# Attention: the probabilities are divided by their sums inside the transpose, as a float32 product with a diagonal matrix

## The chip, the cores and the metric

The kernel runs on one core of a Trainium2 chip. A core has TensorE (PE; its weight loads are listed apart as PEld), VectorE (DVE), ScalarE (ACT), GpSimd (POOL) and SyncE (SP), each with an instruction queue of its own that runs in order, and 16 DMA engines. Two memories matter here: SBUF, and PSUM, into which PE writes. The metric is the time of one execution in device microseconds; the time before is the median of three runs. The profile is one execution, recorded by the hardware profiler.

## The reference, cut to what matters

A trunk of two layers over two request groups, a prompt of 1024 tokens and a sample of 512, with 1024 features: a Fourier mixer and a SwiGLU channel mixer, then grouped-query attention (8 query heads, 2 key heads, 128 features a head) and a second SwiGLU. The change is in the attention, where each row of probabilities is divided by its sum:

```python
def block(qi):
    sc = jnp.einsum('bqkgd,bskd->bkgqs', qi, k).astype(jnp.float32) * scale
    p = jax.nn.softmax(sc, axis=-1).astype(v.dtype)
    return jnp.einsum('bkgqs,bskd->bqkgd', p, v)
```

All is float32, as input and as output.

## The kernel before

The 1536 tokens are three blocks of 512 columns: block 0 is the sample, blocks 1 and 2 are the prompt. Most products are made from operands split into a high and a low part of a reduced format (float32r), in three matmuls (`mm3`, lines 247 to 249: high by high, high by low, low by high). `split` makes the two parts: ACT casts the high part (line 240), and DVE, or POOL where it is told so, subtracts it (line 241). Weights come by SP's DMA queue into `raw` and are split by ACT (line 278) and POOL (line 279).

A few products are left in plain float32: a filler loop of 36 products at the start (line 262), sums over partitions with a column of ones (lines 299 and 1021, four products a time), and `in_rows`, which spreads a column over rows by a product of ones with four diagonal tiles (ACT makes the diagonal from `ident` in line 307, PE multiplies in line 308). Transposes go through PE with `ident` as the moving operand (lines 1003 and 1088).

Two programs are woven together by estimated costs (`weave`): the main one is the channel mixer (`ffn`), whose matmuls are the bulk of the work; the other is attention with its projections. `attend((0,))` runs for the sample and `attend((1, 2))` for the prompt. What the code writes in this woven order is then put into each engine's queue by the framework's scheduler, which may move instructions past each other.

Inside `attend`, for each of 8 heads and each block of 128 query rows (4 blocks a head for the sample, 8 for the prompt, 96 in all):

- `scores` multiplies queries and keys into a PSUM tile `a` (one `mm3` for each 512 keys; one buffer of two banks), takes the row maximum (DVE, line 1070), scales it (DVE, line 1071), makes the exponentials `p` with their row sums (ACT, line 1074), inverts the sums (DVE, line 1075) and multiplies `p` by the inverse in place (ACT, line 1076). `p` has two buffers.
- `turned`, one block later, transposes `p` in pieces of 128x128, four to a PSUM bank `c` (PE, line 1088), and splits the result into `pt` (ACT line 240, DVE line 241). A block has one such group of four for the sample and two for the prompt: 32 x 1 + 64 x 2 = 160 groups, 640 transposes.
- `values`, after every second block, multiplies `pt` with the values (matmuls of 256 columns), copies the result to a tile `t` from the four rotating buffers `tX` (ACT, line 1099) and sends it out by SP's queue (line 1100).

In the profile's names, `g`, `c` and `a` are PSUM banks, `h` and `mid` the mixer's operands, `acc` its accumulators, `col` small columns, and `t` rotating tiles.

Of the kernel before, what the change touches and what calls it, by code (L numbers as in the profile page):

```python
# [13 lines left out]
AF = mybir.ActivationFunctionType  # L14
ALU = mybir.AluOpType
AX = mybir.AxisListType

P = 128
# [106 lines left out]
def trunk_kernel(ctx: ExitStack, tc: tile.TileContext, t: dict):  # L125
    nc = tc.nc
    act, dve, pool, pe, sp = nc.scalar, nc.vector, nc.gpsimd, nc.tensor, nc.sync
# [34 lines left out]
    def tl(name, shape, dt, tag, pool_=None):  # L162
        pool_ = pool_ or pools["sbX" if tag[-1] in "XB" else "sbF"]
        return pool_.tile([P, *shape], dt, tag=tag, name=nm(name), bufs=BUFS[tag])
# [11 lines left out]
    def w_tile(*shape):  # L176
        return tl("w", shape, F32R, "w" + cur[0])
# [4 lines left out]
    def raw_tile(*shape):  # L182
        return tl("raw", shape, F32, "raw" + cur[0])

    def tmp(n=TB, dt=F32):
        return tl("t", [n], dt, "t" + cur[0])

    def bank():
        return tl("c", [TB], F32, "c" + cur[0], pools["ps" + cur[0]])

    def bank2():
        return tl("a", [2, TB], F32, "gX", pools["psX"])
# [14 lines left out]
    def acc_tile(name, shape, dt):  # L207
        return tl(name, shape, dt, "acc", accp)

    def col(n):  # L210
        return cols.tile([P, n], F32, tag=f"col{n}{cur[0]}", name=nm("col"))


    ident = cp.tile([P, P], F32, name="ident")
# [21 lines left out]
    def split(hi, lo, src, gain=None, eng=None):  # L236

        eng = eng or dve
        if gain is None:
            act.copy(hi, src)  # L240
            eng.tensor_tensor(lo, src, hi.bitcast(F32), op=ALU.subtract)  # L241
        else:
            act.activation(hi, src, AF.Copy, scale=gain)
            eng.scalar_tensor_tensor(lo, src, gain, hi.bitcast(F32), op0=ALU.mult, op1=ALU.subtract)

    def mm3(out, lh, ll, rh, rl, first, last):
        pe.matmul(out, lh, rh, start=first, stop=False)  # L247
        pe.matmul(out, lh, rl, start=False, stop=False)  # L248
        pe.matmul(out, ll, rh, start=False, stop=last)  # L249
# [787 lines left out]
    def attend(blocks):  # L1037
        nb = len(blocks)
        T = nb * TB
        nk = T // P  # L1040
        for g in range(NKV):
            kt, vt = w_tile(2, T), w_tile(2, nk, HD)
            kr = raw_tile(T)
            for n, b in enumerate(blocks):
                sp.dma_start(kr[:, n * TB : (n + 1) * TB], dqk[b][NH + g][:, :])
            split(kt[:, 0], kt[:, 1], kr, eng=pool)
            yield 1.0
            vr = raw_tile(nk, HD)
            for n, b in enumerate(blocks):
                sp.dma_start(vr[:, n * 4 : n * 4 + 4], dv[b][g][:, :, :])  # L1050
            split(vt[:, 0], vt[:, 1], vr, eng=pool)
            yield 1.0
            for h in range(g * GROUP, (g + 1) * GROUP):
                qr = raw_tile(T)
                for n, b in enumerate(blocks):
                    sp.dma_start(qr[:, n * TB : (n + 1) * TB], dqk[b][h][:, :])
                qt = w_tile(2, T)
                split(qt[:, 0], qt[:, 1], qr, eng=pool)
                pts = {}

                def scores(qc):
                    qs = slice(qc * P, (qc + 1) * P)
                    sc = bank2()
                    for kb in range(nb):
                        ks = slice(kb * TB, (kb + 1) * TB)
                        mm3(sc[:, kb], qt[:, 0, qs], qt[:, 1, qs], kt[:, 0, ks], kt[:, 1, ks], True, True)
                    s_in = sc[:, 0:nb].rearrange("p b n -> p (b n)")
                    gq = 4 * blocks[0] + qc
                    st = col(3)
                    dve.tensor_reduce(st[:, 0:1], s_in, op=ALU.max, axis=AX.X)  # L1070
                    dve.tensor_tensor(st[:, 1:2], st[:, 0:1], nrqc[:, gq, h : h + 1], op=ALU.mult)  # L1071
                    sm = col(2)
                    p = tl("p", [T], F32, "pX", ap)
                    act.activation(p, s_in, AF.Exp, bias=st[:, 1:2], scale=rqc[:, gq, h : h + 1], accum_out=sm[:, 0:1])
                    dve.reciprocal(sm[:, 1:2], sm[:, 0:1])
                    act.activation(p, p, AF.Copy, scale=sm[:, 1:2])
                    return p

                def turned(qc, p):
                    if qc % 2 == 0:  # L1080
                        pts[qc // 2] = [acc_tile("pt", [2, 4, 256], F32R) for _ in range(nk // 4)]
                    pt = pts[qc // 2]
                    qo = slice((qc % 2) * P, (qc % 2) * P + P)
                    for kq in range(nk // 4):
                        tr = bank()
                        for i in range(4):
                            kc = kq * 4 + i
                            pe.transpose(tr[:, i * P : (i + 1) * P], p[:, kc * P : (kc + 1) * P], ident)  # L1088
                        trv = tr.rearrange("p (i n) -> p i n", i=4)
                        split(pt[kq][:, 0, :, qo], pt[kq][:, 1, :, qo], trv)  # L1090

                def values(u):
                    pt = pts.pop(u)
                    po = bank()
                    for kc in range(nk):
                        mm3(po[:, 0:256], vt[:, 0, kc], vt[:, 1, kc], pt[kc // 4][:, 0, kc % 4], pt[kc // 4][:, 1, kc % 4], kc == 0, kc == nk - 1)
                    n, c0 = divmod(u * 256, TB)
                    o = tmp(256)
                    act.copy(o, po[:, 0:256])
                    sp.dma_start(dot[blocks[n]][:, h, c0 : c0 + 256], o)  # L1100

                last = None
                for qc in range(nk + 1):
                    p = scores(qc) if qc < nk else None
                    yield 0.7 * nb
                    if qc:
                        turned(qc - 1, last)
                        yield 0.8 * nb
                        if qc % 2 == 0:
                            values(qc // 2 - 1)  # L1110
                            yield 0.8 * nb
                    last = p
# [28 lines left out]
    turned = []  # L1141
# [89 lines left out]
    def aux_1():  # L1231
        yield from qkv(0, kept[0])
        yield from attend((0,))
        yield from prepare(2, 0)
# [6 lines left out]
    def aux_3():  # L1241
        yield from paced(qkv(2, kept[2]), 0.4)
        yield from paced(attend((1, 2)), 0.65)
        for b in (1, 2):
            yield from paced(out_projection(b), 0.5)
        close_pool("ap")
        close_pool("sbX")
        tp = open_pool("mT")
        for name in ("B11", "B21", "T2", "T1", "B22"):
            ops[name] = tl(name, [2, 4, TB], F32R, "mT", tp)  # L1250
        yield from moving((1, 2), g_ffn[1], ops)
        close_pool("psX")
        last["pair"] = ffn_pair(1, (1, 2), ops, t["y"])
        cur[0] = "F"
        v = next(last["pair"])
        cur[0] = "X"
        yield v

    last = {}
# [100 lines left out]
```

## Time and profile before

| what | before |
|---|---|
| median of 3 runs (lowest to highest) | 3047.74 us (3045.54 to 3047.97) |
| profiled execution, its own time | 3047.57 us |
| its span, first to last instruction | 3045.8 us |
| mean granted clock of PE | 0.995 |
| line 1074, exponentials, 128x1024 x64 and 128x512 x32 | 77.5 and 24.9 us of ACT |
| line 1075, reciprocals, x96 | 15.2 us of DVE |
| line 240, casts of `pt`, x160 | 88.6 us of ACT |
| line 241, subtractions for `pt`, x160 | 106.9 us of DVE |

The profile's page gives, for each engine, the busy time and its share of the span. The chain of work that ended last follows the last instruction back, step by step, to what released it; its shares say which engine set the end. A row of the table of groups has line, engine, operation, names (out<-in), shapes and count, then busy time, mean duration of one in ns, and the engine's idle time just before these instructions with what ended it. A row of the view of one line or one tile gives a minimum, a median and a maximum in ns. Matmuls overlap in PE's pipeline, so the duration of one is longer than the distance from its start to the next one's.

### The profile page before, as it was taken

How to read it: one execution, taken by the hardware profiler on the slowest of the kernel's cores; microseconds unless marked ns; L12 is line 12 of the kernel's file. 1: busy time of each engine (PE TensorE's matmuls, PEld its weight loads, DVE VectorE, ACT ScalarE, POOL GpSimd, SP SyncE). 2: the span in 40 equal slices, each digit the busy share in tenths (PEclk: the TensorE clock that was granted, in tenths of full speed). 3: DMA queues.
4: the chain of work that ended last, by engine and by line, in shares of the span. 5: the costliest groups of instructions: out<-in, count | busy, mean ns of one | idle time of the engine just before them, and what ended most of it. 6: DMA issues, size and time to landing. Idle time of an engine off the chain costs nothing.

```text
span 3045.8 us, 36762 instructions
## 1 busy us (share of the span) xinstructions
PE 2968.1 (97%) x14184; PEld 2434.7 (80%) x14184; DVE 1666.7 (55%) x2883; ACT 1224.3 (40%) x1758; POOL 1271.5 (42%) x575
## 2 busy tenths in 40 slices
PE   7999999999999999999999999999999999999999
PEld 6778888888877788888878788887787787877777
DVE  7785565534555543533473466565346556555556
ACT  5533332433466522333343577776323222222221
POOL 4334444433333644444433311313537545544452
PEclk8999999999999999999999999999999999999999
DMA  6434543332332734433343211212635411111111
GB/s 222 151 111 136 170 135 99 125 104 77 102 92 94 239 124 136 138 104 101 108 137 108 87 53 52 81 45 97 225 118 196 150 56 49 49 56 56 49 42 63
DMA packets 132079, 330.04 MB, mean 108 GB/s; under 512 B 14176, under 2 KB 28512, under 8 KB 131264
## 3 DMA queue, kind: packets, MB, share of 16 engines
q1 hardware_dynamic: 130688, 318.71, 32.4%
q0 software_dynamic: 928, 7.94, 0.7%
q8 instruction: 111, 1.82, 0.2%
q10 hardware_dynamic: 288, 1.05, 0.1%
q14 instruction: 64, 0.52, 0.1%
HBM read 280.45 MB, written 47.19 MB: 108 GB/s over the span
## 4 chain that ended last, share of the span: by engine, by line
PE 82%; POOL 3%; DVE 3%; DMA 3%; issue 2%; ACT 1%; SPq 0%; POOLq 0%; ACTq 0%; DVEq 0%
PE c L247 12%; PE c L248 12%; PE c L249 12%; PE g L249 10%; PE g L247 10%; PE g L248 10%; PE a L247 5%; PE a L249 4%; PE a L248 4%; PE c L1088 2%; POOL w L279 1%; DVE col L1071 1%; POOL w L241 1%; PE c L1021 1%; POOL h L241 0%
## 5 line engine op out<-in xcount | busy, mean ns | idle before, releaser
L279 POOL TENSOR_TENSOR w<-raw,w 128x1024 fp32r<-128x1024 f32 x354 | 847.2, 2404 | 1304.5 <-ACT w L278 1245.9
L745 DVE TENSOR_TENSOR acc<-c,acc 128x512 f32<-128x512 f32 x704 | 483.2, 689 | 442.1 <-PE c L249 437.9
L278 ACT CAST w<-raw 128x1024 fp32r<-128x1024 f32 x354 | 371.1, 1050 | 570.4 <-PE c L249 274.1
L247 PE MATMUL g<-h,w 128*128 128x512 f32 x1408 | 555.9, 395 | 3.6 <-ACT t L777 3.6
L249 PE MATMUL g<-h,w 128*128 128x512 f32 x1408 | 551.7, 392 | 0.8 <-POOL w L279 0.8
L248 PE MATMUL g<-h,w 128*128 128x512 f32 x1408 | 551.4, 392 | 0.0
L247 PE MATMUL c<-mid,w 128*128 128x512 f32 x1056 | 417.3, 397 | 12.5 <-DVE acc L745 8.4
L248 PE MATMUL c<-mid,w 128*128 128x512 f32 x1056 | 414.3, 392 | 1.7 <-DVE mid L241 1.7
L249 PE MATMUL c<-mid,w 128*128 128x512 f32 x1056 | 413.6, 392 | 0.0
L241 POOL TENSOR_TENSOR w<-raw,w 128x1024 fp32r<-128x1024 f32 (+1 forms) x101 | 228.4, 2267 | 339.6 <-ACT w L240 318.5
L858 DVE TENSOR_TENSOR acc<-c,acc 128x512 f32<-128x512 f32 x352 | 240.9, 690 | 192.2 <-PE c L249 191.5
L247 PEld LDWEIGHTS g<-h,w 128*128 128x128 f32 x1408 | 265.4, 188 | 56.7 <-ACT t L777 4.7
L249 PEld LDWEIGHTS g<-h,w 128*128 128x128 f32 x1408 | 265.2, 188 | 56.3 <-POOL w L279 1.8
L248 PEld LDWEIGHTS g<-h,w 128*128 128x128 f32 x1408 | 265.3, 188 | 52.0
L247 PEld LDWEIGHTS c<-mid,w 128*128 128x128 f32 x1056 | 197.9, 188 | 74.3 <-DVE acc L745 18.3
L248 PEld LDWEIGHTS c<-mid,w 128*128 128x128 f32 x1056 | 198.6, 188 | 42.0 <-DVE mid L241 3.8
L249 PEld LDWEIGHTS c<-mid,w 128*128 128x128 f32 x1056 | 198.6, 188 | 40.4
L248 PE MATMUL c<-h,w 128*128 128x512 f32 x480 | 188.2, 392 | 3.0 <-POOL h L241 3.0
L247 PE MATMUL c<-h,w 128*128 128x512 f32 x480 | 189.1, 395 | 0.0
L249 PE MATMUL c<-h,w 128*128 128x512 f32 x480 | 186.9, 390 | 0.0
L240 ACT CAST w<-raw 128x1024 fp32r<-128x1024 f32 (+1 forms) x101 | 100.2, 1000 | 201.1 <-PE a L249 87.3
L1070 DVE TENSOR_REDUCE col<-a 128x1 f32<-128x1024 f32 (+1 forms) x96 | 100.4, 1046 | 128.0 <-PE a L249 127.8
(342 smaller groups left out, 4769.1 us busy)
## 6 DMA issues: line engine op xcount, KB each, us to landing
raw<-in_down_dram SPq DMA_DIRECT2D x110, 512.0 KB, 3.5
raw<-in_gate_dram SPq DMA_DIRECT2D x88, 512.0 KB, 3.5
raw<-in_up_dram SPq DMA_DIRECT2D x88, 512.0 KB, 3.6
raw<-in_qkv_dram SPq DMA_DIRECT2D x36, 512.0 KB, 3.8
t<-xres SPq DMA_DIRECT2D x56, 256.0 KB, 4.0
raw<-in_wo_dram SPq DMA_DIRECT2D x24, 512.0 KB, 3.6
raw<-in_gate_dram SPq DMA_DIRECT2D x44, 256.0 KB, 2.6
raw<-in_up_dram SPq DMA_DIRECT2D x44, 256.0 KB, 3.1
```

The lines of the kernel that those rows point to most:

```text
L240: act.copy(hi, src)
L241: eng.tensor_tensor(lo, src, hi.bitcast(F32), op=ALU.subtract)
L247: pe.matmul(out, lh, rh, start=first, stop=False)
L248: pe.matmul(out, lh, rl, start=False, stop=False)
L249: pe.matmul(out, ll, rh, start=False, stop=last)
L278: pinned(act.copy(flat[:, 0], raw)) if early else act.copy(flat[:, 0], raw)
L279: pool.tensor_tensor(flat[:, 1], raw, flat[:, 0].bitcast(F32), op=ALU.subtract)
L745: dve.tensor_tensor(acc[dc], ps, acc[dc], op=ALU.add)
L858: dve.tensor_tensor(acc, ps, acc, op=ALU.add)
L1021: pe.matmul(c[:, i : i + 1], sq[:, i * P : (i + 1) * P], ones[:, 0:1], start=True, stop=True)
L1070: dve.tensor_reduce(st[:, 0:1], s_in, op=ALU.max, axis=AX.X)
L1088: pe.transpose(tr[:, i * P : (i + 1) * P], p[:, kc * P : (kc + 1) * P], ident)
```

## The change

After the reciprocal, DVE multiplies `ident` by the column of inverse sums, which gives a diagonal tile `dg` (128x128, one of the `tX` buffers). ACT's pass over `p` is gone. `turned` no longer transposes with `ident`, but multiplies each piece of `p`, as the stationary operand, with `dg` as the moving one: the result is the piece transposed, with each of its columns (a query row) times its inverse sum. It is an ordinary float32 matmul and not PE's transpose.

```diff
                     act.activation(p, s_in, AF.Exp, bias=st[:, 1:2], scale=rqc[:, gq, h : h + 1], accum_out=sm[:, 0:1])
                     dve.reciprocal(sm[:, 1:2], sm[:, 0:1])
-                    act.activation(p, p, AF.Copy, scale=sm[:, 1:2])
-                    return p
-
-                def turned(qc, p):
+                    dg = tmp(P)
+                    dve.tensor_scalar(dg, ident, sm[:, 1:2], None, op0=ALU.mult)
+                    return p, dg
+
+                def turned(qc, p, dg):
...
-                            pe.transpose(tr[:, i * P : (i + 1) * P], p[:, kc * P : (kc + 1) * P], ident)
+                            pe.matmul(tr[:, i * P : (i + 1) * P], p[:, kc * P : (kc + 1) * P], dg, start=True, stop=True)
...
-                        turned(qc - 1, last)
+                        turned(qc - 1, *last)
```

The new diagonal stands on line 1077 and the product on line 1089. The scheduler orders the engines anew. On PE, in the prompt's attention, between the scores of the same two blocks (second head, fourth and fifth block; `a` are the scores, `p` the probabilities, `g` the mixer's products), there stood before:

```order
L249 MATMUL a_14053<-w_13393,w_13920 128x512
L1088 MATMUL c_14076<-ident,p_13996 128x128 x4
L1088 MATMUL c_14083<-ident,p_13996 128x128 x4
L247 MATMUL g_14508<-h_12199,w_14499 128x512
L248 MATMUL g_14508<-h_12199,w_14499 128x512
L249 MATMUL g_14508<-h_12199,w_14499 128x512
L247 MATMUL c_14816<-mid_14489,w_14123 128x512
L248 MATMUL c_14816<-mid_14489,w_14123 128x512
L249 MATMUL c_14816<-mid_14489,w_14123 128x512
```

Behind these come five more matmuls into `g_14508` and then the next scores, `a_14090`. Now the whole gap is, to the first matmul of the next scores `a_14134`:

```order
L249 MATMUL a_14096<-w_13425,w_13960 128x512
L1089 MATMUL c_14120<-t_14041,p_14038 128x128 x4
L1089 MATMUL c_14127<-t_14041,p_14038 128x128 x4
L248 MATMUL g_14172<-h_12231,w_14163 128x512
L249 MATMUL g_14172<-h_12231,w_14163 128x512
L247 MATMUL g_14558<-h_12231,w_14545 128x512
L248 MATMUL g_14558<-h_12231,w_14545 128x512
L249 MATMUL g_14558<-h_12231,w_14545 128x512
L247 MATMUL a_14134<-w_13425,w_13960 128x512
```

The mixer's matmuls between the two blocks' scores go from 11 to 5; the others stand elsewhere in the queue. The same block on DVE, before (`acc` and `pt` as above):

```order
L1070 TENSOR_REDUCE col_14060<-a_14053 128x1
L241 TENSOR_TENSOR pt_14074<-c_14076,pt_14074 128x4x128
L1071 TENSOR_TENSOR col_14060<-col_14060,nrqc 128x1
L241 TENSOR_TENSOR pt_14075<-c_14083,pt_14075 128x4x128
L745 TENSOR_TENSOR acc_12316<-c_14816,acc_12316 128x512
L1075 RECIPROCAL col_14063<-col_14063 128x1
L1070 TENSOR_REDUCE col_14097<-a_14090 128x1
```

And now, with the diagonal tile `t_14110` behind the reciprocal:

```order
L1070 TENSOR_REDUCE col_14103<-a_14096 128x1
L1071 TENSOR_TENSOR col_14103<-col_14103,nrqc 128x1
L241 TENSOR_TENSOR pt_14118<-c_14120,pt_14118 128x4x128
L778 TENSOR_TENSOR g_14172<-g_14172,t_14537 128x512
L1075 RECIPROCAL col_14106<-col_14106 128x1
L1077 TENSOR_SCALAR t_14110<-ident,col_14106 128x128
L241 TENSOR_TENSOR pt_14119<-c_14127,pt_14119 128x4x128
L241 TENSOR_TENSOR mid_14540<-g_14172,mid_14540 128x512
L1070 TENSOR_REDUCE col_14141<-a_14134 128x1
```

The diagonal stands between the reciprocal and the next block's maximum; the scaled maximum moved ahead of the subtraction for `pt`, and a subtraction moved behind the diagonal.

## The prediction, made before the changed kernel ran

> **What bounds the kernel now.** I read the page first: the span, the engines' busy shares, and the chain of work that ended last.
>
> ```profile
> span 3045.8 us, 36762 instructions
> PE 2968.1 (97%) x14184; PEld 2434.7 (80%) x14184; DVE 1666.7 (55%) x2883; ACT 1224.3 (40%) x1758; POOL 1271.5 (42%) x575
> PE 82%; POOL 3%; DVE 3%; DMA 3%; issue 2%; ACT 1%; SPq 0%; POOLq 0%; ACTq 0%; DVEq 0%
> ```
>
> PE is busy for 97% of the span and makes up 82% of the chain; ACT, which the change relieves, is 1% of it. An average can hide a stage with another limit, so next come the two stretches in which attention runs, woven into the channel mixer's matmuls: the sample's (800 to 1000 us) and the prompt's (1690 to 2120 us). The columns are the stretch, its length, then busy time of PE, PEld, DVE, ACT and POOL, the granted clock, the DMA share and GB/s.
>
> ```profile
> 800.00:1000.00 200.00, 194.56 (x995) 158.77 (x994) 118.31 (x209) 130.21 (x214) 74.76 (x35) 1.00 0.32 99
> 1690.00:2120.00 430.00, 413.63 (x2389) 347.00 (x2388) 253.62 (x430) 306.37 (x434) 102.66 (x43) 0.99 0.20 64
> ```
>
> PE is the bound there too: idle for 5.4 of 200 us and for 16.4 of 430 us. ACT is the next busiest (306 of 430 us) but far from full. So a PE instruction added here lengthens the kernel by what it takes, and ACT time saved counts only where PE waits for ACT.
>
> **The products on PE.** Each block of probabilities has its 128x128 pieces transposed in groups of four, one group for each PSUM bank. The rows of line 1088, and of the kernel's plain float32 product of the same shape (line 308: a diagonal tile as moving operand):
>
> ```profile
> L1088 PE MATMUL c<-ident,p 128*128 128x128 f32 x640 | 87.3, 273 | 1.9 <-ACT p L1076 1.9
> L1088 PEld LDWEIGHTS c<-ident,p 128*128 128x128 f32 x640 | 74.1, 140 | 17.7 <-ACT p L1076 6.8 <-DVE pt L241 1.1 <-ACT t L1099 0.3
> L308 PE MATMUL c<-t,ones 128*128 128x128 f32 x136 | 23.4, 302 | 6.3 <-ACT t L307 6.1
> L262 PE MATMUL g<-ones 128*128 128x128 f32 x72 | 9.2, 294 | 0.0
> ```
>
> Line 1088 has 640 records for 640 transposes. Line 262 has 72 records, and the program issues 36 products there: a plain float32 product is two records, each with a weight load of its own, a transpose only one. The changed kernel therefore shows 1280 records where 640 stood. Mean durations overlap in the pipeline, so prices come from the chain, where a piece lasts until the next may run (start, length, what):
>
> ```profile
> 805.99 0.44 PE c L1088 x4
> 1740.58 0.87 PE c L1088 x8
> 738.56 0.48 PE c L308 x4
> 1407.37 0.79 PE c L1021 x8
> 1408.15 0.35 PE c L247
> 1408.50 0.23 PE c L248
> ```
>
> Four transposes cost 0.44 us, eight 0.87 us. Line 1021 issues four float32 products (eight records) in a row, with one moving column: 0.79 us, and the matmul behind them 0.35 instead of 0.23 us, so 0.91 us. Line 308 in groups of two products costs 0.48 us, so 0.96 us for four. I take 0.91, since the new products stand four and eight in a row; 0.96 is the upper end. There are 640 / 4 = 160 groups: 160 x (0.91 - 0.44) = **75.2 us more on PE**, up to 160 x 0.52 = 83.2 us. Nothing hides it, because PE has no more than the idle time above to give. The lower end, a product as cheap as a transpose, is a rival below.
>
> The Trainium skill, "TensorE: Matmul & The Clock Gate", section "Terms", states that transpose mode is four times faster for FP32. It speaks against this change; by it a group would cost 4 x 0.44 = 1.76 us. The rows here show 0.91 / 0.44, about two times, for the product itself, so I keep two and put four among the rivals.
>
> **What ACT loses.** 96 passes over the probabilities and nothing in their place.
>
> ```profile
> L1076 ACT ACTIVATE p<-p,col 128x1024 f32<-128x1024 f32 x64 | 73.9, 1154 | 12.9 <-DVE col L1075 12.9
> L1076 ACT ACTIVATE p<-p,col 128x512 f32<-128x512 f32 x32 | 23.1, 723 | 1.5 <-DVE col L1075 1.5
> ```
>
> That is 97.0 us of ACT. What it is worth is what PE waits for it: by the rows of line 1088 above, 1.9 us of PE and 6.8 us of its weight loads, **8.7 us**, which I take off. Late next in their place is the diagonal tile: exponential, reciprocal, diagonal, without the 1.15 us pass.
>
> **What DVE gains.** 96 diagonal tiles, 128x128 from SBUF to SBUF. Nearest rows: the same operation on 32 and on 512 columns, and line 1071, a one-column operation with both inputs in SBUF (minimum, median, maximum in ns).
>
> ```profile
> L1034 DVE TENSOR_SCALAR rqc<-col x3: 180/181/181, 798.7 to 1709.6; 128x32 f32<-128x32 f32 x3
> L508 DVE TENSOR_SCALAR t<-x_p,r_p x1: 466/466/466, 174.2 to 174.2; 1x512 f32<-1x512 f32 x1
> L508 DVE TENSOR_SCALAR t<-x,r_s x1: 1492/1492/1492, 28.5 to 28.5; 1x512 f32<-1x512 f32 x1
> L1071 DVE TENSOR_TENSOR col<-col,nrqc x96: 149/159/2364, 800.9 to 2110.2; 128x1 f32<-128x1 f32 x96
> L1071 DVE TENSOR_TENSOR col<-col,nrqc 128x1 f32<-128x1 f32 x96 | 50.8, 529 | 1.3
> ```
>
> Between 181 and 466 ns, 128 columns come to 0.181 + 96 x 0.285 / 480 = 0.24 us: an estimate of 23 us for DVE in all. DVE is idle for 176 of the 430 us, and the tile is due only when the next block's scores, six matmuls at 0.23 us, are through; these cover it, so I charge PE nothing. Without that cover it is 0.24 us a block, 23 us. The upper end is line 1071's: a median of 159 ns, a maximum of 2364. Over 96 that is 50.8 - 96 x 0.159 = 35.5 us of being held up. One POOL pass and a held line 1071 stand side by side here:
>
> ```profile
> 805.45 2.40 POOL L279 TENSOR_TENSOR w<-raw,w 128x1024 fp32r<-128x1024 f32 x1 [7.40 <-ACT w L278]
> 805.50 2.36 DVE L1071 TENSOR_TENSOR col<-col,nrqc 128x1 f32<-128x1 f32 x1
> ```
>
> The diagonal tile may be held in the same way. The Trainium skill, "SBUF — State Buffer", section "Who interferes with whom", states that VectorE and GpSimd share a port pair that one of them holds for a whole instruction, and counts `tensor_scalar` among the operations that may take it. The pair of rows above agrees for line 1071, and line 508 (466 against 1492 ns) does not contradict it. By that rule the upper end would be met wherever POOL runs, 102.7 of the 430 us.
>
> The tile also takes one of four rotating buffers that the attention's output tiles use, which leave by SP's queue. An output comes once in two blocks, and its buffer returns four requests later, more than two blocks or 13 us on (430 us for 64 blocks). A transfer of that kind lands in a few us (the last number):
>
> ```profile
> t<-xres SPq DMA_DIRECT2D x56, 256.0 KB, 4.0
> ```
>
> So I charge nothing. A diagonal behind a late transfer would hold DVE, and with it the additions that free PE's banks.
>
> **What moves.** Scores have one PSUM buffer: the next block's may start only when the exponential has read the last. In time:
>
> ```profile
> 1878.73 0.39 PE L249 MATMUL a<-w,w 128*128 128x512 f32 x1
> 1879.16 1.23 DVE L1070 TENSOR_REDUCE col<-a 128x1 f32<-128x1024 f32 x1 [2.44 <-PE a L249]
> 1881.09 1.21 ACT L1074 ACTIVATE p<-a,col,rqc 128x1024 f32<-128x1024 f32 x1 [0.41 <-DVE col L1071]
> 1882.44 0.50 PE L247 MATMUL a<-w,w 128*128 128x512 f32 x1
> PEld a L247 <- ACT p L1074: 21.9, 30, 2.0
> PE a L247 <- ACT p L1074: 11.7, 8, 1.8
> ```
>
> From the last score matmul's start to the next block's first are 3.71 us, 3.48 without that matmul's 0.23. The order before fills them with 11 matmuls and two groups of transposes, 11 x 0.227 + 0.87 = 3.37 us: a wait of 0.1. The changed order has 5 matmuls and two groups of products, 5 x 0.227 + 2 x 0.91 = 2.95 us: a wait of 0.5. Going through all 63 gaps of the second attention in this way, with 3.48 us as what each must hold, the waits come to about 2 us before and 9 us now: **7 us more**. On the other side, an exponential no longer queues behind a pass of line 1076; at most all waits for it in the second attention go, 21.9 + 11.7 = 33.6 us. I take the 7 us and leave the 33.6 to the range.
>
> **The sum.** The profiled execution took 3047.57 us: the span and 1.8 us around it, and 0.2 us under the median of the three runs (3047.74). 3047.6 + 75.2 - 8.7 + 7 = **3121 us**, 2.4% slower.
>
> **Rivals.**
> - *The diagonal is held behind POOL.* If every hold of line 1071's kind reaches PE through late products: 3121 + 35.5 = 3157. It decides only where the products follow their diagonal by less than the hold; for it speaks line 1071, against it that DVE's holds today leave PE 97% busy. One in ten, for 3138 to 3157.
> - *The longer products fill PE's waits.* If all 33.6 us for the exponential vanish, and not 7 more come: 3121 - 33.6 - 7 = 3080. For it: an emptier ACT, and 0.9 us more work in many gaps. Against it: the changed order puts fewer other matmuls there. One in ten, for 3080 to 3104.
> - *A product costs four transposes.* 160 x 1.32 = 211 us, so about 3257. The records of lines 262 and 308 speak against it. 2 in 100.
> - *Faster: p as the stationary operand, loaded once, runs a product in one record.* Then PE gains nothing, the 8.7 us go, and the time is 3039 or less. It decides below 0.44 + 8.7 / 160 = 0.49 us a group. Against it stand three places (lines 262, 308, 1021) where every plain float32 product has two loads. 3 in 100, and 1 in 100 for a price near that point.
>
> **How the numbers follow.** The forecast, 3104 to 3138, has the remaining 74 in 100. The range of 3100 to 3142 takes in a little of the first two rivals and the 83.2 us end. About 0.2% (6 us) is what a measurement of this kernel can tell from no change: slower 0.95, within 0.02, faster 0.03.
>
> **What would show it.** Right: line 1089 with 1280 records, about 0.91 us a group in the chain, and busy about 87 + 75 = 162 us; PE busy near 3043 us and still 97%; ACT near 1127 us; DVE near 1690 us with the diagonal at about 0.24 us; PE's waits for the exponential within 10 us of the old. Wrong: diagonals of 1 to 2 us and PE waiting for them; waits for the exponential gone or doubled; 640 records of line 1089, or a group far from 0.91 us.

## The result, and the profile after

The changed kernel takes 3118.20 us (median of 4 runs, 3115.57 to 3122.43), the kernel before 3047.85 us (4 runs). The ratio is 1.023, with a 95% interval of 1.0216 to 1.0245: slower by 70 us, against 73 us forecast (3121). The profiled execution took 3115.57 us, 68.0 us more than that of before, and so do the spans. First the page of the changed kernel, span and engines:

```profile
span 3113.8 us, 38140 instructions
PE 3035.6 (97%) x14824; PEld 2512.3 (81%) x14824; DVE 1711.5 (55%) x2979; ACT 1135.7 (36%) x1660; POOL 1270.7 (41%) x575
```

PE's busy time grew by 67.5 us, the span by 68.0 us: PE's idle time, span less busy, was 77.7 us and is 78.2 us. ACT lost 88.6 us, and PE's idle time shows no gain from it. The chain on this page was followed back to about 1918 us only, so its shares are not set beside those of before. The second attention is longer: its transposes stood between 1715.8 and 2115.6 us, and the products stand between 1726.4 and 2176.9 us. The two attention stretches after the change, columns as before:

```profile
800.00:1005.00 205.00, 202.79 (x1093) 170.90 (x1093) 122.98 (x238) 109.52 (x178) 72.02 (x34) 1.00 0.29 89
1690.00:2182.00 492.00, 471.42 (x2909) 410.69 (x2908) 294.44 (x505) 238.78 (x373) 100.79 (x43) 0.99 0.18 58
```

In the second, ACT was the next busiest engine with 306 of 430 us and is now at 239 of 492 us, while PE has as little room as before: 20.6 us idle. The groups that answer to those of before, from the view of groups by line:

```profile
L1089 PE MATMUL c<-t,p 128*128 128x128 f32 x1280 | 160.9, 277 | 9.9 <-DVE pt L241 5.5 <-DVE t L1077 4.2 <-ACT mid L240 0.2
L1089 PEld LDWEIGHTS c<-t,p 128*128 128x128 f32 x1280 | 157.6, 193 | 21.9 <-DVE pt L241 7.2 <-ACT pt L240 3.9 <-ACT w L278 1.8
L1077 DVE TENSOR_SCALAR t<-ident,col 128x128 f32<-128x128 f32 x96 | 34.5, 359 | 2.9
L1071 DVE TENSOR_TENSOR col<-col,nrqc 128x1 f32<-128x1 f32 x96 | 50.7, 528 | 3.0
```

There are 1280 records where 640 stood, and the line's busy time went from 87.3 to 160.9 us: 73.6 us. Two groups of products in order of time (start, length of the merged row, instruction):

```profile
1749.53 1.95 PE L1089 MATMUL c<-t,p 128*128 128x128 f32 x16
1751.23 0.48 PE L247 MATMUL g<-h,w 128*128 128x512 f32 x1
1751.55 0.40 PE L248 MATMUL g<-h,w 128*128 128x512 f32 x1
```

From start to start the 16 records take 1.70 us, and the matmul behind them 0.32 instead of 0.23 us: 1.79 us for two groups, 0.90 us each. The view of the probabilities lists who waited for them, and how long in all:

```profile
  PEld a L247: 15.7, 26
  PE a L247: 7.1, 6
```

These are the next scores, waiting for the exponential. In the kernel before, the same view had, with the last two lines for ACT's pass:

```profile
  PEld a L247: 24.5, 36
  PE a L247: 12.5, 9
  PEld c L1088: 6.8, 20
  PE c L1088: 1.9, 3
```

The two kinds of line must not be added. Laid over each other in time, PE's waits fall inside those of its weight loads: 12.53 of the 12.54 us for exponentials before, and 7.08 of 7.09 us now. The loads' waits are therefore the upper bound of what PE loses here, and PE's own are a part of them. What came in place of the waits for the pass stands in the rows of line 1089: the loads wait 7.2 us for the split of the last transposed pieces (5.5 us of it on PE), and PE waits 4.2 us for the diagonal.

### The profile page after: what moved, and what is told of

The parts are those of the page before. It is cut to its first block, busy times and chain, and to the rows that moved or that the text cites. A ratio compares the mean times of both kernels' runs of the same rounds, so it can differ in the third digit from the quotient of the medians.

```text
span 3113.8 us, 38140 instructions
## 1 busy us (share of the span) xinstructions
PE 3035.6 (97%) x14824; PEld 2512.3 (81%) x14824; DVE 1711.5 (55%) x2979; ACT 1135.7 (36%) x1660; POOL 1270.7 (41%) x575
## 5 line engine op out<-in xcount | busy, mean ns | idle before, releaser
L1089 PEld LDWEIGHTS c<-t,p 128*128 128x128 f32 x1280 | 157.6, 193 | 21.9 <-DVE pt L241 7.2
```

What stands on the lines that cost most here:

```text
L1089: pe.matmul(tr[:, i * P : (i + 1) * P], p[:, kc * P : (kc + 1) * P], dg, start=True, stop=True)
```

## The experiments

The ratios below are to runs of the kernel before that were taken beside each group of experiments (medians 3048.54, 3048.45 and 3046.64 us).

### Neither pass nor product

The changed kernel with two edits. Nothing divides the probabilities by their sums any more, so it computes something else than the attention:

```diff
-                    dg = tmp(P)
-                    dve.tensor_scalar(dg, ident, sm[:, 1:2], None, op0=ALU.mult)
+                    dg = ident
...
-                            pe.matmul(tr[:, i * P : (i + 1) * P], p[:, kc * P : (kc + 1) * P], dg, start=True, stop=True)
+                            pe.transpose(tr[:, i * P : (i + 1) * P], p[:, kc * P : (kc + 1) * P], ident)
```

> Leaves the division out: ACT's pass is gone, there is no diagonal, and the pieces are transposed with the identity again. Theory (the time is PE's price of the products, 0.47 us for each of 160 groups, and the freed ACT is worth little): 75 us under the changed kernel, 3043 us, with 3036 to 3048 taken as agreement, 640 records of the transpose. Rival A (the freed ACT is worth much, and the longer products hide part of their price in PE's waits): under 3030. Rival B (most of the 70 us comes from the new order of the queues or from the diagonal on DVE): within 15 us of wherever the product is not the cause, so that the products alone (next run) cost far less than 75 us.

Measured: 3055.91 us (7 runs, 3054.58 to 3059.34), ratio 1.0028 (1.0017 to 1.0039). That is 62 us under the changed kernel, not 75, and **slower than the kernel before, which does more work**. None of the three expectations had this. The rows of the transposes and of the scaled maximum in this kernel, PE's wait for exponentials in front of the next scores, and its waits for DVE's part of the split:

```profile
L1088 PE MATMUL c<-ident,p 128*128 128x128 f32 x640 | 86.6, 273 | 11.0 <-ACT p L1074 11.0
L1071 DVE TENSOR_TENSOR col<-col,nrqc 128x1 f32<-128x1 f32 x96 | 53.7, 559 | 1.6
  PE a L247: 1.0, 1
PE c L247 <- DVE pt L241: 6.3, 4, 1.7
PE c L248 <- DVE pt L241: 1.9, 2, 1.1
```

The transposes need only the exponential now, and PE waits 11.0 us for it right before them, where it waited 1.9 us for the pass. But in front of the next scores it waits 1.0 us and not 12.5, so its waits for the probabilities did not grow: 12.0 us in all, against 14.4. PE's idle time (span less busy) did, from 77.7 to 85.0 us. What grew are the waits of the products with the values (`values`) for DVE's subtraction: 6.3 and 1.9 us on PE, where the kernel before has none. All six of these waits come behind a held line 1071, which keeps the subtraction waiting in DVE's queue. One of them:

```profile
2033.93 2.37 POOL L279 TENSOR_TENSOR w<-raw,w 128x1024 fp32r<-128x1024 f32 x1 [17.49 <-ACT w L278]
2034.02 2.30 DVE L1071 TENSOR_TENSOR col<-col,nrqc 128x1 f32<-128x1 f32 x1
2036.24 0.68 DVE L241 TENSOR_TENSOR pt<-c,pt 128x512 fp32r<-128x512 f32 x1
2036.98 0.39 PE L247 MATMUL c<-pt,w 128*128 128x256 f32 x1 [1.55 <-DVE pt L241]
```

So the freed ACT had to be looked at apart from the product.

### The product, with ACT's pass kept

The kernel before with one edit:

```diff
-                            pe.transpose(tr[:, i * P : (i + 1) * P], p[:, kc * P : (kc + 1) * P], ident)
+                            pe.matmul(tr[:, i * P : (i + 1) * P], p[:, kc * P : (kc + 1) * P], ident, start=True, stop=True)
```

> The kernel before with one edit: the transposes become plain float32 products with the identity. ACT's pass stays, no diagonal is made. Theory: 75 us over the kernel before, 3123 us (3117 to 3130), 1280 records, about 0.91 us a group in the chain; the difference to the changed kernel, some 5 us, is what the freed ACT is worth. Rival A (part of the price hides in PE's waits): 3090 to 3110. Rival B (the diagonal on DVE and the new order are the cost): under 3070.

Measured: 3123.27 us (4 runs), ratio 1.0246 (1.0231 to 1.0261): 74.7 us over the kernel before, as the theory had it. The product alone makes the whole loss. Rivals A and B are out. The changed kernel lies 5.1 us below this one: that is what the freed ACT, the diagonal on DVE and the new order are worth together beside the product. It is a small difference, and the runs of the two kernels overlap (3115.57 to 3122.43 and 3120.33 to 3125.43 us).

### Each product twice

```diff
-                            pe.matmul(tr[:, i * P : (i + 1) * P], p[:, kc * P : (kc + 1) * P], dg, start=True, stop=True)
+                            for _ in range(2):
+                                pe.matmul(tr[:, i * P : (i + 1) * P], p[:, kc * P : (kc + 1) * P], dg, start=True, stop=True)
```

> The changed kernel with each product issued twice, the second writing the same result again. Theory (PE is the bound through both attentions, a record costs 0.112 us): 160 groups x 8 more records x 0.112 = 143 us more, 3261 us (3250 to 3270). Rival (PE's waits for the exponentials, some 23 us, take up part of it): 3235 to 3250. If a product needed only one weight load when it follows itself: 160 x 4 x 0.112 = 72 us, 3190.

Measured: 3246.92 us (4 runs), ratio 1.0651 (1.0633 to 1.0669): 128.7 us over the changed kernel. The engines' row, the products' group and the waits for the probabilities of this kernel:

```profile
PE 3175.7 (98%) x16104; PEld 2660.5 (82%) x16104; DVE 1718.9 (53%) x2979; ACT 1138.7 (35%) x1660; POOL 1271.0 (39%) x575
L1090 PE MATMUL c<-t,p 128*128 128x128 f32 x2560 | 301.9, 275 | 3.8 <-DVE pt L241 2.7 <-DVE t L1077 1.1
  PEld a L247: 7.8, 13
  PE a L247: 3.6, 4
```

The added products cost what the theory gives, 301.9 - 160.9 = 141.0 us of the line, but the loads' waits for exponentials halved, from 15.7 to 7.8 us (PE's own, inside them, from 7.1 to 3.6). The rival's range was met: work put between two blocks' scores hides in part, and here about a tenth did.

### The diagonal on ACT, and the diagonal in buffers of its own

```diff
-                    dve.tensor_scalar(dg, ident, sm[:, 1:2], None, op0=ALU.mult)
+                    act.activation(dg, ident, AF.Copy, scale=sm[:, 1:2])
```

> The changed kernel with the diagonal tile made by ACT (some 0.39 us, as in line 307) and not by DVE. Theory (the diagonal hides behind the next block's scores): within 5 us of the changed kernel. Rival (diagonals held up behind POOL's passes cost PE time): 6 to 13 us faster than the changed kernel, since PE's 5.8 us of waits for the diagonal go and those for the split of the transposed pieces shrink.

```diff
-                    dg = tmp(P)
+                    dg = tl("dg", [P], F32, "dX")
...
-        "gF": 2, "gX": 1, "cF": 2, "cX": 2,
+        "gF": 2, "gX": 1, "cF": 2, "cX": 2, "dX": 2,
```

> The changed kernel with two buffers of its own for the diagonal tile, instead of the four rotating ones that the attention's outputs use too. Theory (a diagonal never waits for an output's transfer): within 3 us of the changed kernel. Rival (diagonals are held by transfers that leave late): 5 us or more faster.

Measured: 3117.16 us with the diagonal on ACT and 3119.95 us with buffers of its own (4 runs each), against 3118.20 us. Ratios are 1.0226 (1.0211 to 1.0241) and 1.0233 (1.0219 to 1.0247), beside 1.023. Neither who makes the diagonal nor which buffers it takes can be seen in the time, as the theories had it. That the diagonal itself costs nothing does not follow. With the diagonal on ACT the loads of the products still wait for it, and for ACT's part of the split:

```profile
L1089 PEld LDWEIGHTS c<-t,p 128*128 128x128 f32 x1280 | 158.6, 194 | 19.7 <-ACT pt L240 7.1 <-ACT t L1077 4.4 <-DVE pt L241 1.6
```

### The pass on DVE

The kernel before with one edit:

```diff
-                    act.activation(p, p, AF.Copy, scale=sm[:, 1:2])
+                    dve.tensor_scalar(p, p, sm[:, 1:2], None, op0=ALU.mult)
```

> The kernel before with one edit: the pass that divides the probabilities is made by DVE (some 0.5 to 1.2 us for 1024 columns) and not by ACT. It separates two things that went together where the division was left out (7 us slower than before): ACT is free, but the probabilities are still finished later than the exponential. Theory (the loss there came from transposes that the scheduler put right behind the scores, where they wait for the exponential; a freed ACT alone is worth little): within 6 us of the kernel before. Rival A (a freed ACT is worth something by itself): 3036 to 3042. Rival B (a freed ACT changes the order for the worse): 3053 to 3060.

Measured: 3055.55 us (8 runs), ratio 1.0029 (1.0018 to 1.0039), 7.1 us slower. The theory fell by its number; rival B's was met. But the run doesn't separate what it was meant to, since a pass on DVE can be held up itself (minimum, median, maximum of its 96 passes):

```profile
L1076 DVE TENSOR_SCALAR p<-p,col x96: 470/753/2589, 804.8 to 2111.0; 128x1024 f32<-128x1024 f32 x64, 128x512 f32<-128x512 f32 x32
  PEld a L247: 27.5, 45
  PE a L247: 12.0, 9
```

The loads' waits for exponentials are 27.5 us here, against 24.5 us before. Counted in the traces of the second attention, what this run and the first have in common is that less work of PE lies between two blocks' scores (by an estimate from the spacing of the matmuls a median of 4.0 and 4.2 us, against 4.7 before), while the exponential ends no earlier: the median way from the last score matmul's start to the exponential's end is 3.7 and 3.6 us, and 3.7 before. That pointed at what makes it long: line 1071.

### The scaled maximum on ACT: a kernel that beats both

The kernel before with one edit:

```diff
-                    dve.tensor_tensor(st[:, 1:2], st[:, 0:1], nrqc[:, gq, h : h + 1], op=ALU.mult)
+                    act.activation(st[:, 1:2], st[:, 0:1], AF.Copy, scale=nrqc[:, gq, h : h + 1])
```

> The kernel before with one edit: the scaled maximum (line 1071) is made by ACT, just ahead of the exponential, and not by DVE. Theory: PE waits some 15 us for exponentials in the attentions because line 1071 stands behind a subtraction on DVE (0.5 us) or is held behind POOL (up to 2.3 us); without it the way from the scores to the exponential's end falls from 3.56 to about 3.1 us and 8 to 12 us go: 3036 to 3041. Rival (the scheduler moves the next scores closer, as it did where the division was left out, and the wait stays): 3045 to 3056.

Measured: 3034.02 us (5 runs, 3032.34 to 3036.28), ratio 0.9953 (0.994 to 0.9965): **14.4 us faster than the kernel before**. In this kernel (the view of line 1071, the waits for the probabilities, and three rows of the timeline):

```profile
L1071 ACT ACTIVATE col<-col,nrqc x96: 282/297/313, 804.4 to 2094.2; 128x1 f32<-128x1 f32 x96
  PEld a L247: 12.6, 35
  PEld c L1088: 4.7, 19
...
1744.31 0.39 PE L249 MATMUL a<-w,w 128*128 128x512 f32 x1
1746.13 0.31 ACT L1071 ACTIVATE col<-col,nrqc 128x1 f32<-128x1 f32 x1
1746.47 1.21 ACT L1074 ACTIVATE p<-a,col,rqc 128x1024 f32<-128x1024 f32 x1
```

On ACT the operation takes 297 ns, longer than DVE's median of 159, but never more than 313, where DVE's took up to 2364. PE itself no longer waits for an exponential (12.5 us before), and its weight loads half as long. With the loads' waits for ACT's pass (6.8 us before, 4.7 now) the loads wait 14.0 us less, about as much as the kernel gains. One number was not met: the way was to fall to about 3.1 us and is 3.37 us in these rows (from the last score matmul's start at 1744.31 us to the exponential's end at 1747.68). What went are the long waits: the longest wait of a load for an exponential was 2.0 us and is 0.5 us. The edit takes away two things at once, which no run separates. In the trace of before, 57 of the 96 scaled maxima stand behind another DVE instruction that came after their maximum, and 28 of the 96 take over 0.4 us beside a POOL pass.

### The same edit in the changed kernel, and without the division

> The changed kernel with the scaled maximum made by ACT. Theory: PE's 9 us of waits for exponentials that are left in the attentions come from line 1071 held behind POOL; 4 to 9 us less than the changed kernel, 3109 to 3114. Rival (the longer products already fill these waits, or the order takes it back): within 3 us of 3118.

> Leaves the division out as the first experiment did, and makes the scaled maximum on ACT. It shows what ACT's pass is worth once exponentials no longer wait for DVE. Theory (the 7 us that leaving the division out cost came from waits for late exponentials, because the new order puts transposes and next scores closer behind the scores): those waits go, and the time is that of the kernel before with the scaled maximum on ACT, 3034, or up to 8 us less. Rival (the new order itself is worse by 7 us, whoever makes the scaled maximum): 3038 to 3045.

The edit in the changed kernel: 3098.46 us (4 runs), ratio 1.0164 (1.015 to 1.0178), 19.7 us under the changed kernel (15.5 us between the spans of the two profiled executions) and more than twice what was expected. Its waits for the probabilities, its products' weight loads and its engines:

```profile
  PEld a L247: 11.2, 35
L1089 PEld LDWEIGHTS c<-t,p 128*128 128x128 f32 x1280 | 156.5, 191 | 15.0 <-DVE pt L241 3.9 <-issue 1.7 <-ACT mid L240 1.5
PE 3034.4 (98%) x14824; PEld 2512.5 (81%) x14824; DVE 1665.3 (54%) x2883; ACT 1160.4 (37%) x1758; POOL 1270.9 (41%) x575
```

PE no longer waits for exponentials, and not they alone come earlier: the loads' waits for the split of the transposed pieces fell from 7.2 to 3.9 us. A held line 1071 holds the subtractions behind it in DVE's queue too, as the rows of the first experiment show, and I had counted only the first of these waits. In the changed kernel 86 of the 96 scaled maxima already stood right behind their maximum, so what the edit takes away here is mostly the holds.

With the division left out and the scaled maximum on ACT: 3030.86 us (5 runs), ratio 0.9944 (0.9931 to 0.9958). Beside the 3034.02 us with the pass, leaving the pass out now gains 3 us, where it cost 7 us with the scaled maximum on DVE. The first experiment's loss is gone, and with it PE's waits for exponentials (12.0 us there) and for DVE's part of the split (8.2 us): neither is left on PE in this trace. The theory's number was met, its account only in part, since what had grown in the first experiment were the waits for the split behind a held line 1071, and not those for exponentials. The order is also a new one here, so an effect of the order of its own is not excluded. The runs of the two kernels with the scaled maximum on ACT were taken at different times and overlap (3026.72 to 3034.43, and 3032.34 to 3036.28), so the 3 us are no firm value: ACT's pass costs this kernel almost nothing.

## Why the prediction was right, point by point

- **The products, 75.2 us.** Right. A group costs 0.90 us in the timeline (0.91 forecast, from line 1021), the line's busy time grew by 73.6 us, and the product alone, with ACT's pass kept, costs 74.7 us. The Trainium skill ("TensorE: Matmul & The Clock Gate", section "Terms") states that transpose mode is four times faster for FP32; by an estimate from it the time would have been 3257 us. Here the transpose is 0.90 / 0.44, two times faster than the product.
- **The freed ACT, 8.7 us off.** The term was too large as a sum: PE's 1.9 us lie inside its loads' 6.8 us, so at most 6.8 us could be had. The waits for the pass did go, but the waits of the products for the split of the last pieces and for the diagonal took their place. Removed alone, the pass brought a loss of 7 us.
- **The moved scores, 7 us more.** This step was wrong in sign. It went through the gaps of the new order with one old way from scores to the exponential, 3.48 us, for all. That gave 2 us of waits for the kernel before, whose rows showed 21.9 us: 23 of its 64 ways in the second attention are longer than 4 us. And the scheduler had also moved the scaled maximum, which I showed in the order of DVE and did not price: it now stands right behind the maximum in 86 of 96 blocks, where it did in 39. In the changed kernel:

```profile
1749.30 0.39 PE L249 MATMUL a<-w,w 128*128 128x512 f32 x1
1749.73 1.23 DVE L1070 TENSOR_REDUCE col<-a 128x1 f32<-128x1024 f32 x1 [2.62 <-PE a L249]
1750.99 0.16 DVE L1071 TENSOR_TENSOR col<-col,nrqc 128x1 f32<-128x1 f32 x1
1751.19 1.21 ACT L1074 ACTIVATE p<-a,col,rqc 128x1024 f32<-128x1024 f32 x1
1752.54 0.50 PE L247 MATMUL a<-w,w 128*128 128x512 f32 x1
```

  The next scores start 3.24 us after the last ones, not 3.71: 3.01 us to fill, where 2.95 us lie in the gap. By the same working the wait of 0.5 us became 0.06 us, and over both attentions the loads' waits for exponentials fell by 8.8 us (24.5 to 15.7, of which PE's own fell by 5.4) instead of rising. How much of this is the moved scaled maximum, and how much the longer products that fill the gaps, no run separates: with the product and the pass they fell too, to 17.0 us, and there 75 of 96 stand right behind their maximum.
- **The two terms together** were -1.7 us in the forecast; the changed kernel is 5.1 us under the one with the product and the pass. Both were mis-sized, in opposite ways, and no run measures one without the other. That their sum was off by only 3 us is luck.
- **The diagonal, nothing.** Right as far as the time can tell: on ACT it makes no difference, but PE does wait 4.2 us for it, and what it costs by itself no run shows. It takes more than the 0.24 us estimated (276/286/1881 ns, 34.5 us in all for 23), and all holds come to 34.5 - 96 x 0.286 = 7.0 us, not the upper end of 35.5. The shared buffers cost nothing that can be seen.
- **The rivals.** Held diagonals did not decide. The longer products do fill waits: doubling them hid some 12 us (141.0 us of PE, 128.7 us of time), so that rival had a mechanism. It had been given 41 us, of which 33.6 us were again PE's and its loads' waits added up; PE was idle for only 16.4 us in that stretch, and the loads' waits alone are 21.9 us. Without the product, freeing ACT costs 7 us, and with it the changed kernel gains 5 us. That about 12 us of the product's price lie in waits that the shorter kernel has anyway is one reading of this; the order of the queues differs too, so it is not shown.

## What to carry to other kernels

Where PE is busy for 97% of the span, price an edit by PE records first: here a plain float32 product is two records and two weight loads, a transpose one, and 97 us saved on ACT could not pay for 74 us on PE. Before freeing an engine, look at what the waits for it really end on: a one-column operation on DVE, which stood behind other DVE work or was held up beside a POOL pass, made the exponentials and the subtractions behind it late, and moving it to ACT was worth 14 us, where leaving out ACT's whole pass was worth 3 us at best. Do not add waits of PE and of its weight loads, which here were the same time seen twice. When a scheduler moves instructions, price every row that moved on the chain in question, not only the gap it leaves.

## What the runs showed of the hardware that was not expected

A DVE operation on one column (line 1071, both inputs in SBUF) takes 0.16 us, or lasts until the POOL pass beside it ends. In the changed kernel 24 of its 96 instances took over 0.4 us; each of these started while a POOL pass ran, and ended within 0.02 us of that pass's end. One of them:

```profile
1810.42 2.38 POOL L241 TENSOR_TENSOR w<-raw,w 128x1024 fp32r<-128x1024 f32 x1 [16.57 <-ACT w L240]
1810.51 2.30 DVE L1071 TENSOR_TENSOR col<-col,nrqc 128x1 f32<-128x1 f32 x1
1812.85 1.20 ACT L1074 ACTIVATE p<-a,col,rqc 128x1024 f32<-128x1024 f32 x1 [2.02 <-DVE col L1071]
1814.20 0.50 PE L247 MATMUL a<-w,w 128*128 128x512 f32 x1 [2.05 <-ACT p L1074]
```

One such hold goes through ACT to PE, which here waits 2.05 us. That DVE may be held while POOL runs was forecast as a bound on the diagonal, from the Trainium skill ("SBUF — State Buffer", section "Who interferes with whom"), and the rows agree with it. Not forecast was what it is worth to take a line that was already there off DVE: 14 us in the kernel before, where only a part is the hold, and 20 us in the changed one.
